# Queries of a sparse-attention block turned by VectorE and the DMA queue instead of TensorE

## The chip, the core and the metric

The kernel runs on one core of a Trainium2 chip. The core has four engines that compute: PE (TensorE, with its weight loads shown apart as PEld), DVE (VectorE), ACT (ScalarE) and POOL (GpSimd). SP (SyncE) does no arithmetic here; it issues most of the DMAs. The metric is the device time of one execution in microseconds (us). Before the change it is 1213.78 us, the median of three runs (1213.2 to 1215.11).

## What is computed

One decoder layer on 1024 tokens of width 1024, all in float32. With the parts that matter here:

```
h = rms_norm(x, g_mix_norm)
z = h @ w_in                                  # q | 6 key/value pieces | gates | 3 conv pieces
q = rms_norm(q.reshape(B, T, 8, 64), g_q)     # each head normed on its own
k_slc, k_win = rms_norm(...);  k_cmp, v_cmp = compress(...)
for each block of 128 tokens, each of 2 groups of 4 heads:
    s = q @ k.T - slope * distance            # three branches: compressed, selected, window
    p = softmax(s) in each branch
    o = g0 * p_cmp @ v_cmp + g1 * p_slc @ v_slc + g2 * p_win @ v_win
x = x + concat(rms_norm(o), rms_norm(conv)) @ w_o
x = x + square(relu(rms_norm(x) @ w_up)) @ w_down
```

With 1024 tokens all 16 blocks of the selected branch are taken, so that branch is plain causal attention.

## The kernel before

**Precision.** Products of float32 operands are made from halves: a value is split into a rounded part (`hi`, type fp32r) and the rest (`lo`), and `mm3` issues hi*hi, hi*lo and lo*hi into one PSUM bank. For the scores the split is stacked on the partitions: for head group g the 64 rows of `half[g]` hold the rounded query and the other 64 rows hold its rest, while `KH[g]` holds the rounded key twice. One matmul over 128 rows (`Qg` by `KH[g]`) then gives q_hi*k_hi + q_lo*k_hi, and a second one (`Qz`, whose other half is zero, by `KL`, the keys' rests) gives q_hi*k_lo.

**Stages.** First x is normed, turned and split. Then come the projections: keys and values, queries, the remaining keys, values and gates, with the compression of keys in between (its weights are loaded as `w1r`, split into `w1h` and `w1l`, and used by the matmuls `hp`). Then the convolution's channels (weights `wcr`, matmuls `zX`, `zZ`, `zW`), half of the output projection (`wc`), the attention in the block order 3, 2, 1, 0, 4, 5, 7, 6, and the MLP (`X`, `Z`, `W`), which begins at about 580 us.

**The queries' way.** In the projection each block of 128 tokens gives `z` (128 tokens x 512 query channels). It is normed by `qri`; then for each group ACT writes the rounded half of `qn` and DVE the rest, each token's row being 8 heads x (64 + 64) values. SP stores this as one 512 KB DMA into the scratch tensor `q_d` (1024 x 1024), in pieces of 4 KB. `qn` has a single buffer. In the attention `queries(tb)` loads for each group 128 x 512 values into `qx` (a single buffer), PE turns the four heads by 128x128 transposes against the identity `ident` into a PSUM tile `tpq` of the ring `pt` (three banks, shared with the transposes of the probabilities), ACT copies this to `Qg`, and POOL sets one half of `Qz` to zero and copies the other from `Qg`. `Qz` is a ring of two.

**The attention.** `scores(tb, g)` makes a head's scores in PSUM; DVE adds the distance penalty and takes the extremum (`nm`), ACT takes exponentials (`pt`, `pc`). POOL multiplies the window and compressed probabilities by `rr` (the ratio of two branches' sums and gates, so that one scale at the end serves all three). `weigh` then turns the probabilities on PE (`tp`), ACT and DVE split them (`ph`, `pl`), and PE multiplies them by the values into `ot`; `oTs`, `ops`, `ot_s` and `osb` turn the result back. The steps of `weigh` for one group are laid between the scores of the next.

**What sets the order.** The program is recorded first: each operation becomes a node, with a cost by engine and size in `Plan.cost`. `Plan.schedule` is a list scheduler: it issues on each engine the ready node of the highest priority (longest way to the end, less a small share of the node's number, plus a bonus `plus`). `Plan.moved` then applies `MOVES`, a table written by hand by node numbers ("these nodes before that one"), and `settled` restores a legal order. Each engine then runs its instructions in that order, and waits in order. DMAs from SP go through eight completion lanes in turn. Since each operation is recorded through a helper, every instruction has the line L268 in the profile, so it is told apart by its tiles.

Of the kernel before, what the change touches and what calls it, by code (L numbers as in the profile page):

```python
# [150 lines left out]
class Plan:  # L151
# [83 lines left out]
    def op(self, name, engine, method, a, kw):  # L235
# [341 lines left out]
def trunk_layer(ctx, tc, x, g_mix_norm, w_in, g_q, g_k, pe_cmp, w_cmp1, b_cmp1, w_cmp2, b_cmp2,  # L577
# [66 lines left out]
    q_d = dram.tile([T, 2 * AW], F32, name="q_d")  # L644
# [164 lines left out]
    with ExitStack() as b1:  # L809
# [131 lines left out]
        for tb, ps in (a for tbs in (QUADS[1], (0,), (1,), (2,), (3,)) for a in z_tokens(pieces, tbs, 512, steps, 1)):  # L941
# [10 lines left out]
            qn = zt.tile([P, H, 2, HD], F32R, name="qn", bufs=1)  # L952
            zh = z.rearrange("p (h d) -> p h d", h=H)
            tt(nc.vector, zh, zh, ri.unsqueeze(2).to_broadcast([P, H, HD]), ALU.mult)
            for g in range(G):
                zg = z[:, g * 256:(g + 1) * 256].rearrange("p (r d) -> p r d", r=R)
                qg = qn[:, g * R:(g + 1) * R]
                copy_act(qg[:, :, g], zg)
                tt(nc.vector, qg[:, :, 1 - g], zg, qg[:, :, g].bitcast(F32), ALU.subtract)
# [26 lines left out]
    with ExitStack() as b2:  # L986
# [319 lines left out]
        for it, tb in [*enumerate(ORDER)][6:] + [*enumerate(ORDER)][:6]:  # L1306
# [26 lines left out]
            if it == 4:  # L1333
                ahead.append(scores(ORDER[0], 1, Qn[1], []))
# [481 lines left out]
```

## Time and profile before

| | |
|---|---|
| time, median of three runs | 1213.78 us |
| span of the profiled execution, first to last instruction | 1212.3 us |
| PE busy | 1202.0 us, 99% |
| DVE, ACT, POOL busy | 917.1, 719.7, 707.2 us |
| granted TensorE clock, mean | 1.000 |
| transposes of queries (`tpq`) | 64, from 289.7 to 497.6 us |

The profiled execution's own time stands as its span: the three timed runs are single executions too, and their median lies 1.48 us above this span. "Busy" of PE counts the time in which at least one matmul is in flight. Matmuls overlap, so the duration of one is longer than the distance between two starts, and a short wait can hide in it. In the timeline the first two columns are start and length in us; a merged row "x4" stands for four instructions, and the brackets at the end give the idle time ahead of it and what ended it. In the view by tile the three numbers are the least, median and greatest duration in ns. In the view by group the numbers after the bar are busy us, mean ns of one, and after the second bar the idle us ahead of the group with what ended it. In the windows view each engine has busy us and the number of its instructions, then come the granted clock, the DMA engines' busy share and GB/s.

### The profile page before, as it was taken

What the parts mean: (1) busy time and instruction counts of PE and PEld (TensorE: products, weight loads), DVE (VectorE), ACT (ScalarE), POOL (GpSimd) and SP (SyncE); (2) the same over time, 40 slices, a digit from 0 to 9 for tenths busy, and PEclk for the clock granted to TensorE, in tenths of its full rate; (3) what the DMA queues carried; (4) which work ended last, traced back from release to release, by engine and by line L of the source; (5) the groups of instructions that cost most, each with busy time, mean ns of one, the idle gap of its engine ahead of it and who ended that gap; (6) DMA issues with size and microseconds to landing.
All of it is one profiled execution on the core that took longest, in us unless ns stands there. A gap on an engine that the chain in (4) does not pass through costs nothing.

```text
span 1212.3 us, 18361 instructions
## 1 busy us (share of the span) xinstructions
PE 1202.0 (99%) x5991; PEld 997.8 (82%) x5991; DVE 917.1 (76%) x1786; ACT 719.7 (59%) x1586; POOL 707.2 (58%) x629
## 2 busy tenths in 40 slices
PE   9999999999999999999999999999999999999998
PEld 6888977778888888888788888888888888888887
DVE  7957867684787898988866556555658898888885
ACT  7577855551588888778856556455335444444441
POOL 2444400011255545335859877777789999989971
PEclk9999999999999999999999999999999999999999
DMA  6375522265121200002234553535539555543513
GB/s 249 79 206 168 169 77 52 60 206 178 42 82 36 70 20 17 28 18 71 87 122 155 176 173 122 182 109 171 190 138 401 163 167 166 177 145 113 175 51 139
DMA packets 104360, 156.06 MB, mean 129 GB/s; under 512 B 20229, under 2 KB 58457, under 8 KB 104265
## 3 DMA queue, kind: packets, MB, share of 16 engines
q1 hardware_dynamic: 98000, 147.06, 37.0%
q10 hardware_dynamic: 5496, 5.28, 1.3%
q0 software_dynamic: 768, 2.56, 0.7%
q8 instruction: 47, 0.77, 0.3%
q14 instruction: 49, 0.39, 0.1%
HBM read 106.63 MB, written 48.23 MB: 128 GB/s over the span
## 4 chain that ended last, share of the span: by engine, by line
PE 93%; ACT 3%; DVE 3%; DMA 1%; issue 1%; POOL 0%; ACTq 0%; DVEq 0%; POOLq 0%
PE X L268 28%; PE Z L268 18%; PE zp L268 9%; PE tp L268 6%; PE zX L268 5%; PE ot L268 5%; PE wa L268 4%; PE W L268 4%; PE wc L268 3%; PE zZ L268 3%; PE zW L268 1%; PE hp L268 1%; ACT ph L268 1%; ACT wu L268 1%; PE tpq L268 0%
## 5 line engine op out<-in xcount | busy, mean ns | idle before, releaser
L268 PE MATMUL X<-we,uu 128*128 128x512 f32 x720 | 202.3, 389 | 0.0
L268 PE MATMUL Z<-we,uu 128*128 128x512 f32 (+1 forms) x582 | 169.1, 387 | 0.0
L268 PEld LDWEIGHTS X<-we,uu 128*128 128x128 f32 x720 | 135.1, 188 | 28.1
L268 ACT ACTIVATE uu<-ur 128x512 fp32r<-128x512 f32 x108 | 66.5, 630 | 116.8 <-PE Z L268 58.3
L268 PEld LDWEIGHTS Z<-we,uu 128*128 128x128 f32 x582 | 108.6, 188 | 22.4
L268 ACT ACTIVATE pt<-pt,nm 128x640 f32<-128x640 f32 (+7 forms) x128 | 93.7, 735 | 17.5 <-DVE nm L268 17.5
L268 PE MATMUL tp<-ident,pt 128*128 128x128 f32 x528 | 102.4, 272 | 0.2
L268 DVE TENSOR_TENSOR y<-X,y 128x512 f32<-128x512 f32 x128 | 86.2, 684 | 20.6 <-PE X L268 20.1
L268 POOL TENSOR_TENSOR d<-d 128x512 f32<-128x512 f32 x64 | 96.1, 1522 | 9.6 <-DVE d L268 7.5
L268 DVE TENSOR_TENSOR pl<-tp,ph 128x512 fp32r<-128x512 f32 (+1 forms) x148 | 94.7, 653 | 7.3 <-ACT ph L268 6.9
L268 ACT ACTIVATE ph<-tp 128x512 fp32r<-128x512 f32 (+1 forms) x148 | 82.4, 575 | 28.5 <-PE tp L268 26.0
L268 DVE TENSOR_TENSOR y<-Z,y 128x512 f32<-128x512 f32 (+1 forms) x97 | 65.3, 679 | 27.1 <-PE Z L268 26.9
L268 POOL TENSOR_TENSOR uu<-ur,uu 128x512 fp32r<-128x512 f32 x54 | 82.3, 1530 | 0.9 <-ACT uu L268 0.7
L268 PEld LDWEIGHTS tp<-ident,pt 128*128 128x128 f32 x528 | 68.5, 140 | 10.5 <-POOL pt L268 0.6
L268 DVE TENSOR_TENSOR we<-s,we 128x512 fp32r<-128x512 f32 x42 | 41.2, 982 | 47.5 <-PE Z L268 19.0
L268 ACT ACTIVATE we<-s 128x512 fp32r<-128x512 f32 x55 | 34.7, 631 | 65.0 <-PE Z L268 36.5
L268 ACT ACTIVATE we<-wu 128x512 fp32r<-128x512 f32 x57 | 36.1, 636 | 54.4 <-PE X L268 39.7
L268 POOL TENSOR_TENSOR we<-wd,we 128x512 fp32r<-128x512 f32 x32 | 52.1, 1628 | 25.1 <-ACT we L268 24.9
L268 POOL IOTA d_sw<- 128x640 f32 (+1 forms) x2 | 1.2, 610 | 107.9 <-PE zZ L268 107.9
L268 DVE TENSOR_TENSOR we<-wu,we 128x512 fp32r<-128x512 f32 x38 | 49.2, 1297 | 18.2 <-PE X L268 9.9
L268 PE MATMUL zp<-w_lo,hTh 128*128 128x512 f32 (+1 forms) x192 | 62.9, 363 | 0.0
L268 POOL TENSOR_TENSOR pt<-pt,rr 128x640 f32<-128x640 f32 (+4 forms) x64 | 62.3, 1004 | 0.0
(1337 smaller groups left out, 3738.3 us busy)
## 6 DMA issues: line engine op xcount, KB each, us to landing
u_d<-d SPq DMA_DIRECT2D x112, 256.0 KB, 4.0
ur<-u_d SPq DMA_DIRECT2D x108, 256.0 KB, 2.8
wu<-in_w_up_dram SPq DMA_DIRECT2D x16, 1024.0 KB, 5.9
wd<-in_w_down_dram SPq DMA_DIRECT2D x16, 1024.0 KB, 7.0
xt<-in_x_dram SPq DMA_DIRECT2D x10, 512.0 KB, 5.4
w_raw<-in_w_in_dram SPq DMA_DIRECT2D x8, 512.0 KB, 5.3
w1r<-in_w_cmp_dram SPq DMA_DIRECT2D x16, 256.0 KB, 2.9
q_d<-qn SPq DMA_DIRECT2D x8, 512.0 KB, 5.1
```

Source lines behind the costliest of these rows:

```text
L268: getattr(engine, method)(*[real(x) for x in a], **{k: real(x) for k, x in kw.items()})
```

## The change

The scratch tensor `q_d` becomes 512 channels x 1024 tokens and holds the queries unsplit and turned. In the projection DVE's `transpose` turns the normed `z` in blocks of 32x32 (`qT`, two buffers): partition 32a + j, column block c then holds channel 32c + j of the tokens 32a to 32a + 31. SP stores it with four DMAs, one for each 32 partitions; a piece is 32 tokens of one channel, 128 bytes. In the attention `query(tb, g)` loads one group with two DMAs, each 64 channels x 4 heads x 128 tokens in pieces of 512 bytes, the same data into both halves of `qx` (two buffers). ACT copies all of it, rounded, to `Qg`; POOL overwrites the half `half[1 - g]` of `Qg` with the rest (unsplit less rounded), and copies the other half to `QZ[g]`. `QZ` is one fixed tile for each group, whose zero half is set once. The queries of a group are asked for right behind the same group's scores of the block before.

The scheduler's cost of the four stores is raised (`plan.drag`), the table of moves is renumbered and shortened, and the scratch of the GpSimd queue's descriptors is set to 8192 bytes.

```diff
     MOVES = (
-        ((3091,), 3192), ((2921,), 2895), ((2731,), 2864), ((3644, 3645, 3646,), 3610), ((3542,), 3411),
...
+        ((2921,), 2895), ((2731,), 2864), ((3628, 3629, 3630,), 3594), ((3526,), 3412), ((3080,), 3041),
...
-    q_d = dram.tile([T, 2 * AW], F32, name="q_d")
+    q_d = dram.tile([AW, T], F32, name="q_d")
...
-            qn = zt.tile([P, H, 2, HD], F32R, name="qn", bufs=1)
             zh = z.rearrange("p (h d) -> p h d", h=H)
             tt(nc.vector, zh, zh, ri.unsqueeze(2).to_broadcast([P, H, HD]), ALU.mult)
-            for g in range(G):
-                zg = z[:, g * 256:(g + 1) * 256].rearrange("p (r d) -> p r d", r=R)
-                qg = qn[:, g * R:(g + 1) * R]
-                copy_act(qg[:, :, g], zg)
-                tt(nc.vector, qg[:, :, 1 - g], zg, qg[:, :, g].bitcast(F32), ALU.subtract)
-            nc.sync.dma_start(q_d[tb * P:(tb + 1) * P], qn.rearrange("p h a d -> p (h a d)").bitcast(F32))
+            qT = zt.tile([P, 16, 32], F32, name="qT")
+            nc.vector.transpose(qT.rearrange("p c i -> p (c i)"), z)
+            plan.drag = 2.7
+            for a_ in range(4):
+                t = tb * P + 32 * a_
+                nc.sync.dma_start(q_d.rearrange("(c j) t -> j c t", j=32)[:, :, t:t + 32], qT[32 * a_:32 * a_ + 32])
+            plan.drag = 1.0
...
-        def queries(tb):
-            Qs = []
-            for g in range(G):
-                qx = kp.tile([P, R, 2, HD], F32, name="qx", bufs=1)
-                q_load.append(nc.sync.dma_start(qx.rearrange("p h a d -> p (h a d)"),
-                                                q_d[tb * P:(tb + 1) * P, g * 512:(g + 1) * 512]))
-                tp = psP.tile([P, 4, P], F32, name="tpq", tag="pt")
-                for r in range(R):
-                    nc.tensor.transpose(tp[:, r], qx[:, r].rearrange("p a d -> p (a d)"), ident)
-                Qg = kp.tile([P, R, P], F32R, name="Qg", bufs=3)
-                Qz = kp.tile([P, R, P], F32R, name="Qz", bufs=2)
-                copy_act(Qg, tp)
-                nc.gpsimd.memset(Qz[half[1 - g]].bitcast(F32), 0.0)
-                nc.gpsimd.tensor_copy(Qz[half[g]], Qg[half[g]])
-                Qs.append((Qg, Qz))
-            return Qs
+        QZ = [kp.tile([P, R, P], F32R, name=f"Qz{g}") for g in range(G)]
+        for g in range(G):
+            nc.gpsimd.memset(QZ[g][half[1 - g]].bitcast(F32), 0.0)
+
+        def query(tb, g):
+            qx = kp.tile([P, R, P], F32, name="qx", bufs=2)
+            for h_ in half:
+                nc.sync.dma_start(qx[h_], q_d[g * R * HD:(g + 1) * R * HD, tb * P:(tb + 1) * P].rearrange(
+                    "(r d) t -> d r t", r=R))
+            Qg = kp.tile([P, R, P], F32R, name="Qg", bufs=3)
+            copy_act(Qg, qx)
+            o = half[1 - g]
+            tt(nc.gpsimd, Qg[o], qx[o], Qg[o].bitcast(F32), ALU.subtract)
+            nc.gpsimd.tensor_copy(QZ[g][half[g]], Qg[half[g]])
+            return Qg, QZ[g]
...
             if it == 2:
-                Qn = queries(ORDER[0])
+                Qn = [query(ORDER[0], g) for g in range(G)]
                 ahead = [scores(ORDER[0], 0, Qn[0], [])]
+                Qn[0] = query(ORDER[1], 0)
             if it == 4:
                 ahead.append(scores(ORDER[0], 1, Qn[1], []))
+                Qn[1] = query(ORDER[1], 1)
...
-                Ps, rr = scores(tb, g, Qs[g], filler) if it else ahead.pop(0)
+                Ps, rr = scores(tb, g, Qn[g], filler) if it else ahead.pop(0)
...
-                if g == 0 and it + 1 < NT:
-                    Qn = queries(order[it + 1])
+                if it and it + 1 < NT:
+                    Qn[g] = query(order[it + 1], g)
...
-    nc = _bacc.Bacc("TRN2", target_bir_lowering=False, num_devices=1)
+    nc = _bacc.Bacc("TRN2", target_bir_lowering=False, num_devices=1, dynamic_dma_scratch_size=8192)
```

How the order of instructions moves is shown at three places. The first is PE in the attention, where the scores of group 1 begin while the products with the window values (`vw`) of the group before still run. Before:

```order
L268 MATMUL ot_5002<-pl_5412,vw_3047 128x512
L268 MATMUL tpq_5458<-ident_68,qx_4995 128x128 x4
L268 MATMUL ops_5409<-ident_68,oTs_5028 128x128
L268 MATMUL s__5470<-KH1_3045,Qg_4931 128x320
L268 MATMUL ops_5409<-ident_68,oTs_5028 128x128
L268 MATMUL s__5470<-KL_3044,Qz_5169 128x320
```

And now, at the answering place of a later block:

```order
L268 MATMUL ot_5490<-ph_5937,vw_3048 128x512
L268 MATMUL ops_5900<-ident_68,oTs_5472 128x128
L268 MATMUL s__5949<-KH1_3046,Qg_5358 128x320
L268 MATMUL ops_5900<-ident_68,oTs_5472 128x128
L268 MATMUL s__5973<-KH1_3046,Qg_5358 128x256
L268 MATMUL ot_5490<-pl_5941,vw_3048 128x512
L268 MATMUL ot_5490<-ph_5959,vw_3048 128x512
L268 MATMUL s__5949<-KL_3045,Qz1_3041 128x320
```

The four transposes `tpq` are gone, and no instruction of PE stands in their place; the product with `Qz1` stands five rows behind the one with `Qg`, two products with `vw` between them.

The second place is POOL in the attention, between two groups' window multiplications (`pt`). Before:

```order
L268 TENSOR_TENSOR pc_4940<-pc_4940,rr_4756 128x256
L268 TENSOR_TENSOR pc_5200<-nm_4790,pc_5200 128x256
L268 MEMSET Qz_5465 64x512
L268 COPY Qz_5465<-Qg_5167 64x512
L268 TENSOR_TENSOR osb_4986<-ot_s_5133 128x2x2x64
L268 TENSOR_TENSOR rffn_61<-rs_t_4933,mhalf_67 128x1
L268 TENSOR_TENSOR rr_4915<-sm_5173,rr_4915 128x4 x2
L268 TENSOR_TENSOR pt_5181<-pt_5181,rr_4915 128x640
```

And now:

```order
L268 TENSOR_TENSOR pc_4892<-pc_4892,rr_4726 128x256
L268 TENSOR_TENSOR rffn_61<-rs_t_4424,mhalf_67 128x1
L268 TENSOR_TENSOR pc_5139<-nm_4742,pc_5139 128x256
L268 COPY Qz0_3042<-Qg_5111 64x512
L268 TENSOR_TENSOR Qg_5358<-qx_4906,Qg_5358 64x512
L268 TENSOR_TENSOR rr_4885<-sm_5177,rr_4885 128x4 x2
L268 TENSOR_TENSOR pt_5121<-pt_5121,rr_4885 128x640
```

The zeroing of `Qz` is gone, and the subtraction into `Qg` stands, with the copy to `Qz0`, between the first step on `pc` and the factors `rr`, on which the multiplications of `pt` wait.

The third place is SP's queue near the end of the query projection. Before:

```order
L268 DMA w1r_1519<-in_w_cmp1_dram 128x2x256
L268 DMA q_d_197<-qn_1432 128x1024
L268 DMA w_raw_1571<-in_w_in_dram 128x2x280
L268 DMA q_d_197<-qn_1546 128x1024
L268 DMA q_d_197<-qn_1638 128x1024
L268 DMA wcr_1730<-in_w_in_dram 128x4x128 x2
```

And now:

```order
L268 DMA w1r_1497<-in_w_cmp1_dram 128x2x256
L268 DMA w_raw_1512<-in_w_in_dram 128x2x280
L268 DMA w_raw_1530<-in_w_in_dram 128x2x280
L268 DMA q_d_197<-qT_1328 32x16x32 x4
L268 DMA q_d_197<-qT_1504 32x16x32 x4
L268 DMA q_d_197<-qT_1583 32x16x32 x4
L268 DMA wcr_1735<-in_w_in_dram 128x4x128 x2
```

Twelve stores stand ahead of the first load of the convolution's weights `wcr`, where two stood behind the last load of `w_raw` before.

More of the change, by code (lines that the diff above doesn't have):

```diff
@@ L1186, in trunk_layer @@
         psS = pool(psS_stack, "psS", bufs=2, space=PSUM)
-        q_load = []
         def scores(tb, g, Qt, filler):
@@ L1465, in trunk_layer @@
         for it, tb in enumerate(order):
-            Qs = Qn
             if it == NT - 2:
```

37 rows, old and new, of the table MOVES are left out of this document.

## The prediction

> **What bounds the kernel now.** I read the page's busy times first, then the chain that ended last, then PE's shortfall by windows of 25 us, then the tile `tpq`. Busy times and the chain:
>
> ```profile
> span 1212.3 us, 18361 instructions
> PE 1202.0 (99%) x5991; PEld 997.8 (82%) x5991; DVE 917.1 (76%) x1786; ACT 719.7 (59%) x1586; POOL 707.2 (58%) x629
> PE 93%; ACT 3%; DVE 3%; DMA 1%; issue 1%; POOL 0%; ACTq 0%; DVEq 0%; POOLq 0%
> ```
>
> PE has a matmul in flight for all but 10.3 us and carries 93% of the chain. So instructions taken from PE should shorten the span, provided that PE does not wait instead. The windows tell where it waits already:
>
> ```profile
> 75.00:100.00 25.00, 24.38 (x135) 20.50 (x134) 17.02 (x29) 18.84 (x74) 12.34 (x9) 1.00 0.42 126
> 100.00:125.00 25.00, 24.55 (x151) 21.74 (x150) 20.84 (x49) 20.17 (x80) 9.16 (x10) 1.00 0.54 176
> 325.00:350.00 25.00, 24.28 (x155) 20.17 (x154) 23.57 (x62) 22.11 (x50) 10.18 (x15) 1.00 0.30 100
> 350.00:375.00 25.00, 24.79 (x150) 20.48 (x149) 21.37 (x76) 21.81 (x57) 13.91 (x24) 1.00 0.19 65
> 375.00:400.00 25.00, 24.63 (x165) 21.07 (x164) 18.62 (x96) 20.82 (x68) 14.86 (x32) 1.00 0.10 33
> 400.00:425.00 25.00, 24.73 (x154) 21.16 (x152) 22.15 (x88) 21.17 (x51) 12.54 (x23) 1.00 0.19 64
> 850.00:875.00 25.00, 25.00 (x112) 20.55 (x111) 17.17 (x16) 9.16 (x16) 20.43 (x15) 1.00 0.46 161
> 325.00:575.00 250.00, 248.39 (x1555) 212.78 (x1554) 219.18 (x737) 206.75 (x470) 113.96 (x177) 1.00 0.13 45
> ```
>
> The columns are the window, its length, then PE, PEld, DVE, ACT and POOL, each busy with its count, the granted clock, the DMA share and GB/s. The clock is 1.00 throughout, so no term for it enters. In the MLP (850 to 875 us) PE is never idle. From 325 to 425 us PE lacks 0.72 + 0.21 + 0.37 + 0.27 = 1.57 us, while DVE and ACT are busy for more than 80% of nearly all of it: that is the first half of the attention, where PE waits for splits and exponentials. Over 325 to 575 us PE lacks 1.61 us in all, so behind 425 us it waits for nothing.
>
> **What is removed from PE.** The tile `tpq`, and two places of PE's timeline:
>
> ```profile
> L268 PE MATMUL tpq<-ident,qx x64: 270/272/302, 289.9 to 497.6; 128*128 128x128 f32 x64
> 452.83 0.60 PE L268 MATMUL tpq<-ident,qx 128*128 128x128 f32 x4
> 453.27 0.27 PE L268 MATMUL ops<-ident,oTs 128*128 128x128 f32 x1
> 344.83 0.60 PE L268 MATMUL tpq<-ident,qx 128*128 128x128 f32 x4
> 345.76 0.50 PE L268 MATMUL ot<-pl,vw 128*128 128x512 f32 x1 [0.34 <-DVE pl L268]
> ```
>
> One transpose lasts 272 ns, but the four that start at 452.83 let the next matmul start at 453.27: 0.44 us for four, 0.11 each. The rest of a duration overlaps its neighbours. 64 x 0.11 = 7.04 us is what PE's queue loses. Not all of it comes back. At 344.83 the four stand just ahead of a wait of 0.34 us for DVE's `pl`: had they not been there, `ot` would still have waited for `pl`. The lack of 1.57 us says how common that is; 48 of the 64 lie from 325 us on:
>
> ```profile
> 325.00:575.00 250.00, 8.05 (x48) 5.90 (x48) 7.11 (x12) 1.00 0.13 45
> ```
>
> (the same columns, of `tpq`'s instructions alone: PE, PEld, ACT). I take two such groups of four and one transpose more as saving nothing, an estimate: 9 x 0.11 = 1.0 us. Its bounds are none (7.04 us come back) and all 48 (5.28 us are lost).
>
> **The projection.** Removed are 16 copies of ACT (405 ns) and 16 subtractions of DVE (515 ns); added are 8 transposes of DVE over 128x512.
>
> ```profile
> L268 ACT ACTIVATE qn<-z 128x256 fp32r<-128x256 f32 x16 | 6.0, 405 | 1.5 <-DMA q_d<-qn 1.2 <-DVE z L268 0.4
> L268 DVE TENSOR_TENSOR qn<-z,qn 128x256 fp32r<-128x256 f32 x16 | 8.1, 515 | 2.3 <-ACT qn L268 2.3
> L268 DVE TENSOR_TENSOR z<-z,qri 128x512 f32<-128x512 f32 x8 | 5.5, 690 | 0.2
> L268 DVE COPY hT<-tp 128x256 f32<-128x256 f32 x2 | 0.9, 426 | 0.9 <-PE tp L268 0.9
> ```
>
> No 32x32 transpose of DVE is in the trace. The nearest rows are the multiplication of the same 128x512 tile (690 ns) and a one-source copy of half as many elements (426 ns, so at most 852 for the whole). I take 690; DVE then loses 16 x 0.515 - 8 x 0.690 = 2.7 us of work and ACT 6.5 us, and even at 852 DVE loses 1.4 us. Neither is the bound there (17.02 and 18.84 of 25 us in the first window), so I count nothing for it, gain or loss. One wait does go. `qn` has a single buffer, and at 98.87 the chain runs through its store:
>
> ```profile
> 98.87 5.10 DMA q_d<-qn
> 105.59 0.39 PE L268 MATMUL hp<-w1h,ah 128*128 128x256 f32 x1 [0.45 <-ACT w1h L268]
> ```
>
> ACT waits for the store, and `w1h`, queued behind on ACT, makes PE wait 0.45 us. `qT` has two buffers and ACT no part in it any more: -0.45 us, bounded by 0 and by the two windows' whole lack of 1.07.
>
> **The stores.** Eight of 512 KB become 32 of 64 KB, each 512 pieces of 128 bytes. The rows nearest to one such store:
>
> ```profile
> q_d<-qn SPq DMA_DIRECT2D x8, 512.0 KB, 5.1
> k_d<-krow SPq DMA_DIRECT2D x32, 64.0 KB, 2.3
> L268 SPq DMA_DIRECT2D q_d<-qn x8: 338/339/614, 82.1 to 134.2; - x8
> L268 SPq DMA_DIRECT2D k_d<-krow x32: 513/586/652, 38.8 to 156.4; - x32
> 129.07 4.96 SPq L268 DMA_DIRECT2D wcr<-in_w_in_dram  x7
> 135.54 0.50 ACT L268 ACTIVATE wcr<-wcr,cols 128x256 f32<-128x256 f32 x1
> ```
>
> Landing should lie between 2.3 us (a store of `k_d`, as many bytes in larger pieces) and 5.1 (one of eight times the bytes). The first load of `qx` is issued at 262 us, over 120 us behind the last store, so this hides under the whole of the convolution's projections. Issuing costs SP 32 x 0.586 = 18.8 us in place of 8 x 0.339 = 2.7, and the one place where that could tell is ahead of the loads of `wcr`: 12 stores x 0.586 = 7.0 us stand there where two took 0.7, so 6.3 us later at worst. The seven loads issued from 129.07 on are used from 135.54 on. I count nothing, since SP reaches that place after waiting for the data of the stores and most stores go out as blocks finish; the bound stands among the rivals.
> By the Trainium skill's "DMA: Bandwidth & Descriptors", section "Specifications", a transfer under 512 bytes falls below line rate because of a read-modify-write, which speaks against 128-byte pieces. No trace here shows such pieces; by that rule the stores would be slower, and the sum the same as long as those 120 us cover them.
>
> **The attention.** ACT's copy to `Qg` stays (593 ns on average from PSUM); from SBUF a copy of the same size, `w1h`, takes 618 ns, so nothing. POOL's part changes:
>
> ```profile
> L268 POOL CAST Qz<-Qg 64x512 fp32r<-64x512 f32 x13 | 7.9, 608 | 18.4 <-PE s__3945 L268 7.1 <-PE s__6319 L268 2.2 <-ACT Qg L268 1.8
> L268 POOL MEMSET Qz<- 64x512 f32 x13 | 6.8, 521 | 5.9 <-PE s__4596 L268 3.9 <-PE s__5445 L268 1.5
> L268 POOL TENSOR_TENSOR pt<-pt,rr 128x512 f32<-128x512 f32 x4 | 5.0, 1290 | 0.0
> L268 POOL TENSOR_TENSOR uu<-ur,uu 128x512 fp32r<-128x512 f32 x54 | 82.3, 1530 | 0.9 <-ACT uu L268 0.7
> L268 POOL TENSOR_TENSOR rr<-sm,rr 128x4 f32<-128x4 f32 x30 | 5.4, 202 | 30.0 <-DVE sm L268 21.8 <-ACT pt L268 7.0 <-DVE nm L268 1.1
> ```
>
> A zeroing of 0.52 us goes and a subtraction over 512 elements comes: 1.29 (the multiplication `pt` of that width) to 1.53 us (`uu`, a subtraction with a rounded result). I take 1.29: +0.77 us for each query group, 14 x 0.77 = 10.8 us over those that fall within the attention. What hides it is POOL's idle time ahead of `rr`: 30.0 us over 15 pairs, 2.0 us each, in which POOL waits for DVE's sums. POOL is busy for 114 of 250 us. So I count nothing; without that cover it is the full 10.8 (the rival on POOL). The scores need `Qg` complete about 0.85 us later than before, but `query` is now asked for a whole group's turn earlier. The loads double in number on SP, at 0.6 us at most, and no longer wait for PE to empty the one `qx`, which held SP for long:
>
> ```profile
> SPq L268 <- PE tpq L268: 108.2, 9, 33.9
> ```
>
> With two buffers a load waits instead until ACT's copy and POOL's subtraction of the group two before are done, a whole turn earlier. The loads of weights queued behind it on SP can therefore start sooner, which only helps them.
>
> **Sum.** -7.04 + 1.0 - 0.45 = -6.49 us, against a span of 1212.3 us that lies 1.48 below the median of 1213.78. The median should fall alike: **1207.3 us**. The bounds of these terms (the transposes' 1.0 between 0 and half of 5.28, the `qn` wait between 0 and 1.07) give the forecast's own range, 1204 to 1210.
>
> **The rivals.**
>
> *More comes back.* The `tpq` tiles shared the three banks of ring `pt` with the transposed probabilities, so a `tpq` put a `tp` one turn later. If the lack of 325 to 425 us goes with them: -7.04 - 0.45 - 1.57 = -9.1, 1204.7 us. For it: the lacks lie where `tpq` lies. Against: the reason shown at 345.76 is DVE, not a bank.
>
> *Nothing much comes back.* If DVE and ACT pace the attention, the 48 transposes from 325 us on filled time that PE has anyway. Then 16 x 0.11 + 0.45 = 2.2 us is left: 1211.5 us. For it: DVE 219.18 and ACT 206.75 of 250 us, and an order tuned by many small moves that is now recast with fewer of them. Against: PE's lack behind 425 us is almost zero, so PE, not DVE, sets the pace there.
>
> *POOL becomes the bound: slower.* The subtraction waits for ACT's copy, and with POOL's copy it stands directly ahead of `rr` and the window multiplications, which PE's `tp` of the window wait for. At the tightest place now
>
> ```profile
> 397.06 0.61 POOL L268 CAST Qz<-Qg 64x512 fp32r<-64x512 f32 x1 [0.70 <-ACT Qg L268]
> 397.63 0.35 POOL L268 TENSOR_TENSOR rr<-sm,rr 128x4 f32<-128x4 f32 x2
> ```
>
> `rr` follows with no gap. If each group pays its 0.77 us in full, 10.8 - 6.5 = +4.3: 1218.1 us. The sign turns where more than 6.49 / 14 = 0.46 us per group is uncovered. Against it: the 2.0 us of idle time per pair.
>
> *The stores delay `wcr`.* 6.3 us later, less the slack: the loads go from 129.07 on, a transfer of that queue lands 2.3 to 5.1 us after its issue, and the first use is at 135.54, so 1.4 to 4.2 us are free. That leaves 2.1 to 4.9 us of wait, 3.5 in the middle: 1210.8 us.
>
> *Each transpose was worth its whole duration.* 64 x 0.272 = 17.4: 1196.4 us. Against it stand the four starts in 0.44 us.
> The Trainium skill's "TensorE: Matmul & The Clock Gate", section "Part 4: PE-mode transpose", gives about 275 ns for one in a kernel; the trace agrees on the duration (272 ns), and shows that it isn't the price.
>
> That the change leaves the transposes on PE is excluded by the order.
>
> **How the numbers follow.** Forecast 0.46, more 0.18, nothing much 0.20, POOL 0.11, stores 0.03, whole durations 0.02. The predicted time is the forecast's. 0.2% (2.4 us) is about what a measurement of this kernel can tell from no change: faster is below 1211.35, slower above 1216.2. The first, second, fifth and sixth cases are faster, 0.69. "Nothing much" lies by the bound, its estimate leans on a shared wait, and I give all but 0.01 of it to no change: 0.19. Slower is 0.12. The range takes in the forecast, the second case and most of the third, and leaves out the slower case and the sixth: 1202 to 1214.
>
> **What would show each step.** Right: no `tpq`, PE busy near 1195 us, an unchanged lack from 75 to 425 us but for 0.45 at 105 us, and rows that start about 6.5 us earlier from the MLP on. The subtraction `Qg<-qx,Qg` at 1.3 us with idle time left ahead of `rr`. Wrong: PE idle for DVE `pl` or ACT in the attention by several us more (nothing much), PE's `tp` waiting for POOL `pt` or the scores for POOL `Qg` (POOL), PE waiting ahead of `zX` at 135 to 140 us (stores), or stores of over 100 us to landing.

## The result and the profile after

The changed kernel takes 1222.17 us (1221.36 to 1223.49); the kernel before takes 1214.44 us beside it. The ratio is 1.0067, with a 95% interval of 1.0053 to 1.0082: 8 us slower, where 6.5 us less was forecast. The page after (span, busy times, chain that ended last):

```profile
span 1220.8 us, 18259 instructions
PE 1199.1 (98%) x5927; PEld 990.1 (81%) x5927; DVE 915.8 (75%) x1778; ACT 714.5 (59%) x1570; POOL 719.6 (59%) x631
PE 87%; DVE 6%; ACT 4%; issue 1%; DMA 1%; POOL 0%; SPq 0%; ACTq 0%; DVEq 0%; POOLq 0%
```

PE's time with a matmul in flight fell by 2.9 us, but the span grew by 8.5, so PE is idle for 21.7 us where it was idle for 10.3. PE's share of the chain went from 93% to 87%; DVE took 6% and ACT 4%. The windows of 25 us and the one over the attention (columns as in the prediction), first one of before that stood full, then those after:

```profile
150.00:175.00 25.00, 25.00 (x109) 19.76 (x108) 16.32 (x41) 15.32 (x41) 2.53 (x5) 1.00 0.31 80
```

```profile
75.00:100.00 25.00, 23.52 (x129) 19.29 (x128) 13.52 (x24) 13.65 (x58) 11.26 (x8) 1.00 0.50 112
100.00:125.00 25.00, 24.62 (x141) 21.18 (x140) 20.51 (x41) 19.88 (x80) 10.55 (x9) 1.00 0.66 147
150.00:175.00 25.00, 21.75 (x102) 17.43 (x101) 15.00 (x44) 16.37 (x50) 5.71 (x8) 1.00 0.36 91
325.00:350.00 25.00, 24.18 (x146) 19.53 (x144) 23.40 (x62) 21.20 (x47) 13.43 (x17) 1.00 0.25 74
350.00:375.00 25.00, 22.64 (x132) 18.72 (x132) 19.83 (x67) 19.83 (x51) 15.44 (x24) 1.00 0.26 85
375.00:400.00 25.00, 24.04 (x149) 19.85 (x147) 19.39 (x90) 21.21 (x63) 14.50 (x25) 1.00 0.08 22
400.00:425.00 25.00, 23.59 (x136) 18.93 (x135) 20.18 (x89) 20.90 (x60) 13.24 (x26) 1.00 0.15 48
325.00:575.00 250.00, 243.05 (x1474) 204.01 (x1473) 217.28 (x740) 202.67 (x463) 122.35 (x177) 1.00 0.12 39
```

There are two new losses. From 150 to 175 us PE was never idle and now lacks 3.25 us. In the attention it lacks 6.95 us of 250, where it lacked 1.61. The same matmuls by their tiles, before and after, show where the delay builds up (three durations in ns, then first and last start):

```profile
L268 PE MATMUL hp<-w1h,ah x32: 277/281/386, 79.2 to 121.2; 128*128 128x256 f32 x32
L268 PE MATMUL zW<-hTh,wcul x24: 387/394/412, 155.9 to 258.8; 128*128 128x512 f32 x24
L268 PE MATMUL ops<-ident,oTs x64: 270/272/329, 338.4 to 582.8; 128*128 128x128 f32 x64
```

```profile
L268 PE MATMUL hp<-w1h,ah x32: 274/282/386, 80.5 to 123.3; 128*128 128x256 f32 x32
L268 PE MATMUL zW<-hTh,wcul x24: 387/394/398, 159.8 to 265.1; 128*128 128x512 f32 x24
L268 PE MATMUL ops<-ident,oTs x64: 270/272/329, 342.6 to 590.3; 128*128 128x128 f32 x64
```

PE is 1.3 us late at the first `hp`, 2.1 at the last, 6.3 at the end of the convolution, 4.2 at the first `ops` and 7.5 at the last; the MLP adds half a microsecond. So the start, the projection and the convolution lose 6.3 us. Of the first 1.3 us, 1.2 are there at 20 us already, before any work of the change. Between 265 and 340 us some 2 us come back. The attention from there on loses 3.3 us although 48 transposes (5.3 us by their distance) are gone from it. Four of PE's waits, each with what ended it:

```profile
91.59 0.39 PE L268 MATMUL hp<-w1l,ah 128*128 128x256 f32 x1 [1.22 <-DVE w1l L268]
156.53 0.50 PE L268 MATMUL zX<-t2h,wcuh 128*128 128x512 f32 x1 [1.10 <-ACT ta L268]
167.21 0.51 PE L268 MATMUL zX<-hTh,wcuh 128*128 128x512 f32 x1 [2.15 <-ACT wcuh L268]
357.85 0.50 PE L268 MATMUL wa<-w_hi,mh 128*128 128x512 f32 x1 [1.32 <-DVE ml L268]
```

And SP's queue ahead of the convolution, with ACT's use of the last load in it:

```profile
121.22 11.81 SPq L268 DMA_DIRECT2D q_d<-qT  x12
133.15 4.25 SPq L268 DMA_DIRECT2D wcr<-in_w_in_dram  x7
142.11 0.86 SPq L268 DMA_DIRECT2D wcr<-in_w_in_dram  x1
145.99 1.71 ACT L268 ACTIVATE wcr<-wcr,cols 128x256 f32<-128x256 f32 x4 [2.56 <-DMA wcr<-in_w_in_dram]
```

Seven loads of `wcr` begin 4.1 us later than before, the eighth 6.6 us later (142.11 for 135.54). ACT then waits 2.56 us for it.

### The profile page after: what moved, and what is told of

It is laid out like the page before. It is cut to its first block, busy times and chain, and to the rows that moved or that the text cites. A ratio compares the mean times of both kernels' runs of the same rounds, so it can differ in the third digit from the quotient of the medians.

```text
span 1220.8 us, 18259 instructions
## 1 busy us (share of the span) xinstructions
PE 1199.1 (98%) x5927; PEld 990.1 (81%) x5927; DVE 915.8 (75%) x1778; ACT 714.5 (59%) x1570; POOL 719.6 (59%) x631
## 3 DMA queue, kind: packets, MB, share of 16 engines
q0 software_dynamic: 768, 2.56, 0.8%
## 4 chain that ended last, share of the span: by engine, by line
PE 87%; DVE 6%; ACT 4%; issue 1%; DMA 1%; POOL 0%; SPq 0%; ACTq 0%; DVEq 0%; POOLq 0%
PE X L268 28%; PE Z L268 18%; PE zp L268 8%; PE zX L268 5%; PE tp L268 5%; PE ot L268 4%; PE wa L268 4%; PE W L268 4%; PE wc L268 3%; PE zZ L268 2%; DVE pl L268 2%; PE zW L268 1%; DVE pt L268 1%; PE hp L268 1%; ACT pt L268 1%
```

## The experiments

Three theories stood after the comparison. **Order**: the new way of the queries is worth its 6.5 us, and the recast order of the instructions loses 15. **Data path**: POOL's subtraction, the stores or the loads cost more than they were given, in any order. **Filler**: the transposes were worth next to nothing, since DVE and ACT pace the attention.

To hold the order fixed while the work changes, several kernels take each engine's instructions from a list, not from priorities; the list is the order of one of the two kernels, with left-out instructions struck from it. The edit in the planner, which the runs below share except `b_short`, `a_wcr` and `a_defer` (these change only the table of moves):

```diff
-                if ready[e]:
-                    t = free[e]
-                elif wait[e]:
-                    t = max(free[e], wait[e][0][0])
-                else:
+                if e not in ORDERS or turn[e] == len(ORDERS[e]) or ORDERS[e][turn[e]] not in there:
                     continue
+                n = nodes[ORDERS[e][turn[e]]]
+                t = max(free[e], there[n.k])
...
-        return end, self.moved(order)
+        return end, self.settled(sorted(order, key=lambda n: place[n.k]))
```

The last line came in only after the first runs: it also fixes the order in which tiles are set up, and in which ACT's loads stand among its arithmetic. In `b_noturn`, `b_pool` and `a_nosub`, and in the three runs next below, tiles were still set up in another order.

### The changed kernel in the order of the kernel before

`a_border`:

> The changed kernel, every engine bound to the order of the kernel before: 64 transposes fewer, the subtraction right ahead of the copy into Qz, four stores where one stood. Theory 'order': the new way of the queries is worth its 6.5 us, and the loss (start 1.2, projection 1.5, the wait for wcr 3.5, attention 8 us) came from the recast order: 1206 to 1210 us. Rival 'data path': POOL's subtraction, the loads and the stores of 128 bytes cost what they cost in any order: 1218 us or more. Rival 'filler': DVE and ACT pace the attention, so the transposes were worth about nothing: 1211 to 1215 us.

1223.11 us, ratio 1.0081 (1.0054 to 1.0109).

`a_early`, only nodes ahead of the attention in that order:

> The changed kernel, with only the work before the attention (start, projections, convolution) in the order of the kernel before; the attention in its own new order. 'Order': the 6.3 us that the changed kernel is behind at 264 us go, less up to 1.5 for the more numerous stores: 1216 to 1217.5 us. 'Data path': the wait for wcr comes from twelve stores on SP and stays at 3.5 us: 1219 us or more.

1220.64 us, 1.0063 (1.0042 to 1.0083).

`a_late`, only the attention and what follows:

> The changed kernel, with only the attention and what follows in the order of the kernel before. 'Order': the attention of the changed kernel gains only 7.04 less 8.3 us, so 8.3 us come back: about 1214 us. 'Data path' (POOL's subtraction ahead of rr): unchanged, 1221 to 1223 us. 'Filler': 3 to 5 us come back, 1217 to 1219 us.

1227.02 us, 1.0101 (1.0086 to 1.0116). All three missed "order", but their profiles were late before anything of the change begins: in `a_border`, PE is 4.2 us behind at 20 us. The lateness begins at the top of ACT's timeline in `a_border` (start, duration, and in brackets the wait and what ended it):

```profile
0.75 1.28 ACT L268 ACT_TABLE_LOAD   x1 [0.75 <-PEq L1771]
1.49 0.58 ACTq L268 DMA_DIRECT2D rows<-in_g_mix_norm_dram  x1
```

in the chain of waits of `a_border` (start and duration of the transfer):

```profile
1.49 4.50 DMA rows<-in_g_mix_norm_dram
```

and in the chain of the kernel before:

```profile
0.76 2.04 DMA rows<-in_g_mix_norm_dram
```

My list had put ACT's loading of its table ahead of the first DMA that it issues, and the transfer lasted 4.50 us in place of 2.04. That the one made the other is not shown, since the tiles were set up in another order too. So these runs settle nothing on the change. They were made again with the last line of the diff:

> As a_border, with the tiles set up and ACT's first loads issued as in the kernel before (a_border was 4.2 us late at 20 us, in work that the change doesn't touch). a_border less 4.2: 1218 to 1219 us. 'Order' as first held: 1206 to 1210 us.

1219.18 us, 1.0047 (1.0032 to 1.0062), as expected from `a_border` less its late start. "Order" as first held falls: in the order of the kernel before, the changed work is still 5.2 us slower. The recast order costs the rest, 1222.17 - 1219.18 = 3.0 us. That size is rough: the intervals of the two ratios overlap, and each against its own runs of the kernel before makes it 2.6 us.

`a_early2`, `a_early` made again in that way:

> a_early without the faults of its start: the changed kernel with start, projections and convolution in the order of the kernel before, the attention in its own. The changed kernel is 6.3 us behind at 264 us, a_bord2 only 1.8; if that part of the order is all that lies between them: 1217 to 1218 us. If the two orders of the attention differ too: a_bord2's 1219.2 or more.

1219.62 us, 1.0043 (1.0026 to 1.006): by the medians 2.6 us of those 3.0 lie ahead of the attention. The profiles don't bear out so sharp a split: at 262 us `a_early2` is 3.3 us behind the kernel before and `a_bord2` 1.7, though both have the same order up to there.

### What the shortened table costs the kernel before

`b_short` takes from the table of the kernel before the 30 moves that the change dropped:

```diff
     MOVES = (
-        ((3091,), 3192), ((3378,), 3453), ((3374,), 3377), ((402, 410, 411,), 207), ((188,), 395),
...
```

> The kernel before with the 30 moves taken out of its table that the change dropped, nothing else. It moves 36 instructions of PE, most of them in the first 25 us. If the dropped moves are what costs 1.2 us at the start and 1.5 us in the projection: 1216 to 1217 us. If the start alone: 1215.2 us. If neither: 1214 us.

1217.57 us, 1.0028 (1.0018 to 1.0037): 3.3 us, more than expected, in its profile 0.6 at the start and 2.3 between 320 and 440 us. A table tuned by hand on one program carries some 3 us of it. It need not be the same loss as the changed kernel's: the shortened table costs the kernel before most in the attention, the new order of the changed kernel, as far as the medians tell, ahead of it.

### The transposes alone

`b_noturn` and `b_noturn2` leave PE's transposes out of the kernel before, in its order. `b_noturn2` also gives `qx` two buffers and takes the changed kernel's size of the descriptors' scratch, which the lines below don't show:

```diff
-                tp = psP.tile([P, 4, P], F32, name="tpq", tag="pt")
-                for r in range(R):
-                    nc.tensor.transpose(tp[:, r], qx[:, r].rearrange("p a d -> p (a d)"), ident)
...
-                copy_act(Qg, tp)
+                copy_act(Qg, qx.rearrange("p h a d -> p h (a d)"))
```

> The kernel before, every engine in its own order, with the 64 transposes tpq and their PSUM tile left out: ACT copies qx as loaded into Qg, so the scores are of queries that are not turned. Nothing else changes. The prediction's first term (PE sets the pace, 64 x 0.11 us): 1206 to 1208 us. 'Nothing much comes back' (DVE and ACT pace the attention): 1210 to 1212 us.

1219.92 us, 1.0048 (1.0032 to 1.0064): slower with less work. In its chain, ACT's second copy waits for a load that the single `qx` had held back until the first copy:

```profile
399.55 3.93 DMA qx<-q_d
```

> As b_noturn, with two faults of that run mended: qx has two buffers (with one, ACT's second copy waited 3.9 us for a load), and the tiles are set up in the order of the kernel before (b_noturn and b_pool lost 1.5 us near 65 us, where they do nothing new). PE sets the pace: 1206 to 1208 us. DVE and ACT pace the attention: 1210 to 1213 us. If it is still slower than 1214, then PE's transposes paid for themselves in some way that no theory here has.

1212.7 us, 0.9989 (0.998 to 0.9998): all 64 transposes gone, and 1.3 us saved. The kernel before, unchanged but bound to its list, was not run. In the profiles `b_noturn2` is 0.4 us late at 20 us already, and its attention gives about 0.9 us back, so 1 to 2 us is as well as the worth of the transposes is known. The number of "filler" holds; its cause is tried below. Three waits of PE in the timeline of `b_noturn2`:

```profile
327.54 0.39 PE L268 MATMUL s__3628<-KH,Qg 128*128 128x256 f32 x1 [0.60 <-DVE nm L268]
338.76 0.50 PE L268 MATMUL ot<-ph,vs 128*128 128x512 f32 x1 [0.51 <-ACT ph L268]
346.80 0.50 PE L268 MATMUL ot<-pl,vw 128*128 128x512 f32 x1 [0.69 <-DVE pl L268]
```

and its window over the attention, columns as above:

```profile
325.00:575.00 250.00, 245.07 (x1514) 207.98 (x1512) 220.24 (x741) 207.64 (x472) 114.19 (x177) 1.00 0.13 45
```

PE's idle time here went from 1.61 to 4.93 us. The third row is the wait that the prediction quotes at 345.76: 0.34 us with the transposes ahead of it, 0.69 without. Most of what PE no longer did, it waited, and by the trace most of these waits end with DVE (`nm` 1.9 us, `rr` 0.9, `pl` 0.7; ACT's `ph` 0.8).

`b_twice` makes each transpose twice, one right behind the other:

```diff
-                    nc.tensor.transpose(tp[:, r], qx[:, r].rearrange("p a d -> p (a d)"), ident)
+                    for _ in range(2):
+                        nc.tensor.transpose(tp[:, r], qx[:, r].rearrange("p a d -> p (a d)"), ident)
```

> The kernel before, in its own order, with each of the 64 transposes tpq made twice, one right behind the other. If PE sets the pace where they stand: 64 x 0.11 = 7.0 us more, 1221 us. If they fill time in which PE waits anyway, the mirror of b_noturn2: 1 to 2.5 us more, 1215.5 to 1217 us.

1219.64 us, 1.0045 (1.003 to 1.006): 5.5 us more, so 0.086 us for each transpose added against 0.02 for each taken away. My mirror fell: PE has next to nothing free either. The time lies between the two cases, so neither holds in full.

```profile
325.00:575.00 250.00, 248.77 (x1578) 214.63 (x1575) 216.13 (x735) 203.26 (x463) 111.92 (x174) 1.00 0.13 45
```

PE is idle for 1.23 us of 250: the added work had only 1.61 us of idle time to go into.

`b_nopl` takes DVE's subtraction `pl` away instead:

```diff
-                split_psum(ph, pl, tp)
+                copy_act(ph, tp)
+                tt(nc.vector, pl[:, 0, 0:8], tp[:, 0, 0:8], ph[:, 0, 0:8].bitcast(F32), ALU.subtract)
...
-                    nc.tensor.matmul(o, v, pl, start=False, stop=last and i == len(vs) - 1)
+                    nc.tensor.matmul(o, v, ph, start=False, stop=last and i == len(vs) - 1)
```

> The kernel before, in its own order, with DVE's subtraction pl cut to 8 elements a partition in the attention, and PE's second product with each ph taken with ph again (the rests of the probabilities are left out). PE's work stays as it is, DVE loses some 75 us of it. If DVE's splits set the pace of the attention, PE's starts from 262 to 500 us lose a good part of the 12 us by which they lie wider than the work asks: 1204 to 1209 us. If PE sets the pace: 1213 to 1214 us.

1212.39 us, 0.9985 (0.9976 to 0.9995): 1.8 us less, though DVE lost 60 us of work in this window (219.18 before):

```profile
325.00:575.00 250.00, 248.68 (x1566) 213.99 (x1565) 159.26 (x741) 207.65 (x474) 115.54 (x178) 1.00 0.13 46
```

The time lies below both of its cases. DVE's splits aren't what holds PE here: with them gone PE is as full as before. Taking work from PE alone or DVE alone gives 1 to 2 us. That fits several limits of nearly the same length, the second of which begins where the first is relieved; it isn't shown. Which one stands behind PE isn't told apart. Since PE is 99% busy in `b_nopl`, DVE may still be the next limit once PE is relieved, as the waits of `b_noturn2` suggest. The transposes and `pl` were not left out together, and ACT (203 to 208 of 250 us in all three windows) and the waits from engine to engine were not taken away.

### POOL's subtraction

`b_pool` and `b_pool2` put a subtraction in the place of POOL's zeroing. It reads one operand twice and took 1.04 us, where the changed kernel's takes 1.29, so it adds 0.52 us to the zeroing and not the 0.77 that was meant:

```diff
-                nc.gpsimd.memset(Qz[half[1 - g]].bitcast(F32), 0.0)
+                o = half[1 - g]
+                zero = ident[o].unsqueeze(1).to_broadcast([HD, R, P])
+                tt(nc.gpsimd, Qz[o], zero, zero, ALU.subtract)
```

> The kernel before, in its own order, with POOL's zeroing of Qz made by a subtraction of the same 64 x 512 elements (1.29 instead of 0.52 us, the same place in POOL's queue). If POOL's idle time ahead of rr covers it, as the prediction took: 1213 to 1215 us. If POOL's queue decides: up to 0.77 us for each of 14 groups, 1217 to 1224 us.

1218.86 us, 1.0034 (1.0021 to 1.0047), of which a part is not POOL's: its profile is 1.5 us late at 70 us already.

> As b_pool, with the tiles set up in the order of the kernel before, so that the 16 operations of POOL are the only difference. Covered by POOL's idle time: 1213.5 to 1215 us. As b_pool's own attention, where its profile lost 1.2 us: 1215 to 1216. POOL decides fully: 1217 us or more.

1215.7 us, 1.0015 (1.0006 to 1.0025): 1.7 us, the middle case, for an operation that was too short. Over half of the loss in its profile, 0.95 us, comes between 262 and 285 us: while POOL's first two subtractions run there, DVE's `MCl` at 266.74 us takes 1.55 us where the next one takes 0.68, and PE then waits 0.77 us for DVE's `hTl`. That is not POOL's queue. In the attention it isn't the cause of the 8 us: DVE's `pl` takes 682 ns before and 683 after. `a_nosub` and `a_nosub2` cut the subtraction in the changed kernel, in its own order:

```diff
-            tt(nc.gpsimd, Qg[o], qx[o], Qg[o].bitcast(F32), ALU.subtract)
+            tt(nc.gpsimd, Qg[o, 0, 0:8], qx[o, 0, 0:8], Qg[o, 0, 0:8].bitcast(F32), ALU.subtract)
```

> The changed kernel, in its own order, with POOL's subtraction into Qg cut to 8 elements a partition; the rest of that half stays the rounded value. If the subtraction is what makes the attention slow: 5 us less or more, 1214 to 1217 us. If the pace comes from DVE and ACT: 1220 to 1222 us.

1227.92 us, 1.0113 (1.0096 to 1.013). In its chain PE waited for one load of `xt`, whose transfer lasted 10.49 us. Tiles were set up in another order here too, and nothing is learned of the subtraction.

> As a_nosub, with the tiles set up in the order of the changed kernel (a_nosub lost 6 us at one load of xt at 284 us, which has nothing to do with the subtraction). Subtraction decides: 1214 to 1217 us. DVE and ACT pace the attention: 1220.5 to 1222.5 us.

1222.15 us, 1.0067 (1.0052 to 1.0082): no different from the changed kernel. The order that its planner made lays the subtraction where it costs nothing. The same cut in `a_bord2`:

> a_bord2 with POOL's subtraction cut to 8 elements a partition (the rest of that half stays the rounded value). If the 2.0 us that a_bord2 lost at 400 us are the subtraction ahead of rr: 1217 to 1217.5 us. If they come from the load or ACT's copy: 1219 us.

1216.9 us, 1.0021 (1.0012 to 1.0031): 2.3 us less, at the place expected. POOL and PE of `a_bord2` there:

```profile
400.20 1.29 POOL L268 TENSOR_TENSOR Qg<-qx,Qg 64x512 fp32r<-64x512 f32 x1 [0.80 <-POOL osb L268]
401.55 0.60 POOL L268 CAST Qz<-Qg 64x512 fp32r<-64x512 f32 x1
402.12 0.35 POOL L268 TENSOR_TENSOR rr<-sm,rr 128x4 f32<-128x4 f32 x2
```

```profile
402.87 0.33 PE L268 MATMUL tp<-ident,pt 128*128 128x128 f32 x1 [0.54 <-POOL pt L268]
407.23 0.44 PE L268 MATMUL tpo<-ident,osb 128*128 128x128 f32 x2 [1.58 <-POOL osb L268]
```

The subtraction stands ahead of `rr` and of the `osb` behind it, and PE waits for both: 2.1 us at one place. So this cost belongs to the place in the queue, not to the operation.

### The stores in SP's queue

`a_wcr` puts the first eight loads of `wcr` ahead of the last four of the twelve stores, by one more move:

```diff
+        ((1963, 1964, 1970, 1971, 2117, 2118, 2124, 2125,), 1311),
```

> The changed kernel with one move more: the first eight loads of wcr stand ahead of the last four of the twelve stores, so SP issues them while it would wait for the third block's data (from about 127 us instead of 133 to 142). If the late eighth load of wcr makes PE wait at 150 to 165 us: 3.5 us less, 1218.7 us. If something else makes ACT or PE late there (the DVE transposes, the order of ACT): 1222 us.

1223.23 us, 1.0075 (1.0058 to 1.0092): nothing gained. The loads are early now, but PE is late at the same place. Pieces of its chain from 135 to 151 us, the transfers and what they release:

```profile
135.17 4.80 DMA q_d<-qT
...
143.70 2.02 DMA k_d<-krow
...
145.81 0.13 DVE krow L268
...
148.76 1.93 DMA v_dw<-vrow
...
150.71 0.03 ACT vrow L268
```

SP now issues the stores of `k_d` and `v_dw` late, which hold the buffers of `krow` and `vrow` that DVE and ACT need next. `a_defer` therefore moved the stores of the last two blocks behind those:

```diff
+        ((1311, 1312, 1313, 1314, 1412, 1413, 1414, 1415,), 2275), ((1971,), 1653),
```

> The changed kernel, with the eight stores of the last two query blocks moved on SP behind the stores of k_d and v_dw and ahead of the next loads of wcr, and the eighth load of wcr one place earlier. If the small stores in SP's queue cost the 3.5 us at 150 to 165 us (they hold wcr, and the buffers of krow and vrow, and by those ACT): 1218 to 1219 us. If the small stores only move a wait that comes from ACT or DVE: 1221 to 1223 us.

1224.36 us, 1.0084 (1.0069 to 1.0099): nothing gained again; the eight stores then stand ahead of the next `wcr`. `a_one` makes a block's four stores as one:

```diff
-            for a_ in range(4):
-                t = tb * P + 32 * a_
-                nc.sync.dma_start(q_d.rearrange("(c j) t -> j c t", j=32)[:, :, t:t + 32], qT[32 * a_:32 * a_ + 32])
+            nc.sync.dma_start(q_d[64 * tb:64 * tb + 64].rearrange("r (s x) -> (r s) x", s=2),
+                              qT.rearrange("p c i -> p (c i)"))
```

> The changed kernel in its own order, each block's four stores made as one DMA of 128 pieces of 2 KB at the place of the first (the scratch then holds the queries in another layout, and the loads read them permuted). If the 24 additional DMAs in SP's queue make the wait of 3.3 us at 150 to 175 us and some of the 1.5 us at 75 to 125 us: 1217 to 1219 us. If the data of the stores are late, however many they are: 1221 to 1223 us.

1220.59 us, 1.0053 (1.0038 to 1.0068): 1.6 us less, between the two cases. By time alone this isn't clear of noise, since its interval overlaps that of the changed kernel. PE's first wait at 150 to 170 us is gone, the second is as it was:

```profile
164.80 0.50 PE L268 MATMUL zX<-hTh,wcuh 128*128 128x512 f32 x1 [2.15 <-ACT wcuh L268]
```

So the stores make the first: `a_one` has a quarter of them, and pieces of 2 KB in place of 128 bytes, and doesn't tell the two apart. The second belongs to the new order. In the changed kernel ACT scales four `wcr` ahead of the `wcuh` that PE waits for, where the kernel before scales one (0.51 us at 161.19):

```profile
164.95 1.69 ACT L268 ACTIVATE wcr<-wcr,cols 128x256 f32<-128x256 f32 x4
```

`a_bord2`, with all 32 stores, has the first wait alone:

```profile
153.33 0.50 PE L268 MATMUL zX<-t2h,wcuh 128*128 128x512 f32 x1 [1.53 <-ACT ta L268]
```

The stores cost at a second place in `a_bord2`. Four of them hold SP for 2.89 us where the kernel before has one of 0.34, the next load of `w1r` is issued at 101.76 us in place of 100.03, and PE waits:

```profile
98.77 2.89 SPq L268 DMA_DIRECT2D q_d<-qT  x4
105.68 0.38 PE L268 MATMUL hp<-w1h,ah 128*128 128x256 f32 x1 [0.93 <-ACT w1h L268]
```

With the stores made as one this order was not run.

## Why the prediction was wrong

**The first term failed**: "64 x 0.11 = 7.04 us is what PE's queue loses", with 1.0 us given back at places where PE waits anyway. For work added, the distance of 0.11 us is a fair price, if a high one (0.086 in `b_twice`). Taken away, the 64 gave 1.3 us, so 5.7 us were given back, not 1.0. The error is in the sentence that takes PE's lack of 1.57 us as a measure of how many transposes stand ahead of a wait. Idle time tells how much more work fits in. It doesn't tell how soon the next limit comes when work is taken out: a wait that the transposes covered exactly shows as no idle time at all. The wait for `ph` at 338.76 us is such a one: 0.51 us in `b_noturn2`, none before. "Behind 425 us it waits for nothing" was the same misreading: of the 16 transposes from 430 to 500 us, 1.76 us, `b_noturn2` got 0.8 us back.

**The rival "nothing much comes back" named the mechanism.** Its 2.2 us for what comes back stand against 1.3 measured for the transposes. Its cause, DVE's pace, isn't confirmed: the new waits of `b_noturn2` name DVE most, but `b_nopl` took DVE's splits away with PE still full.

**POOL.** The price was right (1.29 us a subtraction: 1272 to 1310 ns), and so was the tight place. The step "I count nothing, 2.0 us of idle time per pair" failed as an average: in the old order one place of two subtractions at 400 us paid 2.3 us. The rival's 10.8 us were far too many, and in the changed kernel's own order the subtraction cost nothing.

**The stores.** The groups of instructions on their tiles in the changed kernel, with the transpose on DVE and POOL's subtraction (three durations in ns, first and last start):

```profile
L268 DVE STREAM_TRANSPOSE qT<-z x8: 694/704/714, 80.3 to 135.1; 128x512 f32<-128x512 f32 x8
L268 SPq DMA_DIRECT2D q_d<-qT x32: 303/488/1630, 81.1 to 143.6; - x32
L268 POOL TENSOR_TENSOR Qg<-qx,Qg x16: 1272/1290/1310, 278.4 to 504.8; 64x512 fp32r<-64x512 f32 x16
```

and the page's list of DMA issues in the changed kernel, with the us from issue to landing at the end:

```profile
q_d<-qT SPq DMA_DIRECT2D x32, 64.0 KB, 2.7
k_d<-krow SPq DMA_DIRECT2D x32, 64.0 KB, 2.8
```

The transpose (704 for 690 ns), the issue (488 for 586) and the landing (2.7 us, within 2.3 to 5.1) came out as costed. "I count nothing" for SP failed, and the rival that was given 0.03 had one of the places: the eighth `wcr` was 6.6 us late, and PE waited 1.10 us there (the 2.15 us behind it come with the new order). Its cause was too narrow. Loading `wcr` early gained nothing, since the stores of `k_d` and `v_dw` stand in SP's queue there too. Nor is `wcr` the only load: in `a_bord2` `w1r` is late as well.
By the Trainium skill's "DMA: Bandwidth & Descriptors", section "Specifications", transfers under 512 bytes fall below line rate. Pieces of 128 bytes landed no later here than `k_d`'s, but both are below that bound, so the runs don't test it; what cost time was the issuing.

**The `qn` wait** (-0.45 us) is gone in the changed kernel, but in the order of the kernel before the wait at that place grew to 0.93 us (105.68 in `a_bord2`), so the term's gain isn't shown. The window from 75 to 100 us lacks 1.48 us now, 1.22 of it at 91.59 for DVE's `w1l`. In part that is the new order's: the kernel before waits 0.62 us for `w1l` at 92.91, and in `a_bord2` the window is full. But in `a_early2`, which has the same order there, it lacks 1.45 us.

```profile
75.00:100.00 25.00, 25.00 (x138) 21.18 (x137) 15.39 (x26) 17.38 (x71) 13.05 (x9) 1.00 0.54 121
```

**SP's later loads** were to start sooner. They don't: SP waits for POOL to empty `qx` (113.0 us in the list of waits after, below) as long as it did for PE (108.2 us), since the loads are still asked for well ahead.

```profile
SPq L268 <- POOL Qg L268: 113.0, 11, 20.7
```

**What wasn't in the prediction** is the order itself. It said that an order recast with fewer moves speaks for no gain, but gave it no price. It is about 3.0 us from `a_bord2` to the changed kernel, with the wait for `wcuh` (2.15) and part of that for `w1l` (1.22) in it. Two more things in the forecast were loose: its range of 1204 to 1210 is wider than its own bounds give (1205.7 to 1209.4), and it had no term for the start of the program.

**The sum.** 3.0 us for the order, 2.3 for the subtraction and about 1.6 for the stores, less 1.3 for the transposes, make 5.6 of the 8 us. The subtraction and the stores were measured in different orders, so the terms needn't add. Each is a difference of medians whose intervals reach 1 to 2 us either way, so the sum is known no better than that. About 2.4 us stay open. In `a_bord2` 0.4 us of lateness are there at 20 us, and one more wait, absent before, stands ahead of the attention:

```profile
296.02 0.50 PE L268 MATMUL wc<-hTh,MCh 128*128 128x512 f32 x1 [0.88 <-DVE xt L268]
```

The loads of `qx`, the start and the layout of the buffers were not tried alone.

## What to carry to other kernels

When the busiest engine is 99% busy in an order tuned by hand, work taken from it may bring little back, here 1.3 of 7.04 us: measure that first, by leaving the work out with the order held fixed, beside the unchanged kernel in the same fixed order, and then add the same work a second time. Price each issue in a DMA queue by what stands behind it there, not by when its own data are needed. A change to a program whose order was tuned by hand also pays for a new order, here about 3 us of 1214; holding the old order fixed shows how much of a loss is that.

## What the runs showed that was not expected

- The response of PE isn't even: 64 transposes more cost 5.5 us, 64 fewer save 1.3.
- Nothing but the order in which tiles are set up, and in which ACT's loads stand among its arithmetic, parts `a_border` from `a_bord2`: 1223.11 and 1219.18 us. The one difference that I could name is ACT's table load ahead of its first DMA.
- A kernel that did less was slower: in `b_noturn` the single-buffered `qx` put a load of 3.93 us ahead of ACT's copy. The order in which its tiles were set up had a part in it (1.5 us at about 65 us), and the two were mended together.
